# Hybrid decoder block on one Trainium2 core: the PEER gate table's one-hot products in two fp32r passes, with the row-building work shared out anew

## The chip, the cores and the metric

The kernel runs on 1 core of one Trainium2 chip. The metric is the device time in microseconds (us) of one execution. The engines are PE (matmul; PEld is its weight load), DVE (vector), ACT (scalar), POOL (GpSimd) and SP, which issues DMAs.

## The reference, cut to what matters

The block has a mixing sub-layer (projection, gated convolution, windowed attention, output projection) and a channel sub-layer, PEER: every token and each of 8 heads picks 16 of 128 x 128 experts by a product key, softmaxes their scores into gates, and sums the picked experts.

```python
top, pos = lax.top_k(cand, PEER_TOPK)
eidx = jnp.take_along_axis(cidx, pos, axis=-1)       # expert = 128 * ia + ib
g = jax.nn.softmax(top, axis=-1)
a = jax.nn.gelu(jnp.einsum('thkd,td->thk', u_tab[eidx], ht))
return jnp.einsum('thk,thkd->td', g * a, v_tab[eidx])
```

Sizes: 1024 tokens, width 1024, 16384 experts, all in float32. For a token the 8 x 16 = 128 picks are 128 triples (ia, ib, g).

## The kernel before, in words

The 1024 tokens go through the front (norms, projections, attention, output projection, key scores, top 16) in three groups of 384, 384 and 256 tokens (`front`). The first 640 tokens (five tiles of 128) get their experts densely: all 16384 experts are multiplied with the tokens, and a table of gates weights them (`dense`). The last 384 tokens gather their rows by indirect DMA on POOL's queue (`gather`).

`spread` (L714) makes the gate table of one tile of 128 tokens. Its inputs are three [token, pick] arrays, which PE transposes (L720) into PSUM `gps`, so that a pick lies on a partition and a token in a column; ACT copies them to `tr` (L722). For token t the 128 x 128 table is one matmul over the picks: the weights `oi` hold, for pick p, the gate g at column ia; the moving operand `oj` holds a 1 at column ib. A **step** handles four tokens; a tile has 32 steps, the five tiles have 160.

- `make(k)` builds `oi` for four tokens and one `oj` of 4 x 128 columns on DVE (L742). The four tokens' `oi` go by the pattern `HOT = "APVV"`: one on ACT in two instructions (L735, L736), one on POOL and two on DVE, each in one instruction (L738) that compares the column numbers `iota` with ia and multiplies by g. There are 8 `oi` buffers, two steps' worth.
- `multiply(k)` is four fp32 matmuls of 128 columns into one of two PSUM buffers `gps` (L750). The trace shows an fp32 matmul as two records, so a step has 8.
- `evict(k)` copies `gps` to `stage` on ACT (L756); after 8 steps a DMA sends it to DRAM `gd` (L758).

The steps of `spread` are background work. `front` calls `bg(us)` in each half of a projection (L296), which hands out steps at `SPREAD = 0.94` per us of projection time; the tiles of the first group are made in the second group's front, those of the second group in the third's, and whatever is left is drained at a front's end, before the next begins. A tile's steps stand between two `select` passes, which find the picks of a tile and are mainly DVE work. Each engine takes its instructions in one fixed order, which a scheduler sets when the program is built: an instruction that waits holds up all behind it on its engine. On POOL the same queue holds the subtractions that make the low parts of the attention's k and q (`kL` L410, `qL` L418) and of the mixed output (`mc` L402).

The core of the step before:

```python
for x in range(4):
    oi = gb.tile([P, P], F32, name="oi", bufs=8)
    who = pat[t % len(pat)]
    ...
        (G if who == "P" else V).tensor_scalar(oi, iota, tr[:, 0, t:t + 1], tr[:, 2, t:t + 1],
                                               op0=ALU.is_equal, op1=ALU.mult)
```

Of the kernel before, what the change touches and what calls it, by code (L numbers as in the profile page):

```python
# [21 lines left out]
P = 128  # L22
# [4 lines left out]
PH = 8  # L27
# [20 lines left out]
GT = 3  # L48
J = 4
TB = 32  # L50
HOT = "APVV"
RATE0, RATE = 0.0, 0.49
ORDER = True
BACK = 0
# [20 lines left out]
def hymba_peer_kernel(ctx: ExitStack, tc: tile.TileContext, a, out: bass.AP):  # L75
# [65 lines left out]
    vpv = t1.tile([P, P], F32, name="vpv")  # L141
    upv = t1.tile([P, 4, 2], F32, name="upv")
    V.memset(upv, 0.0)
    stat = t1.tile([P, 5, P], F32, name="stat")
    nc.sync.dma_start(stat, a["stat"])
    back = t1.tile([P, 5, P], F32, name="back")
    nc.sync.dma_start(back, a["back"])
# [196 lines left out]
    def group_stats(chunks, T):  # L344
        pt = pj.tile([P, TM], F32, name="pj")
        for i, src in enumerate(chunks):
            sq = tmp("sq")[:, 0:T]
            A.activation(sq, src, AF.Square)
            PE.matmul(pt[:, 0:T], stat[:, i, :], sq, start=(i == 0), stop=(i == len(chunks) - 1))
        r = tp.tile([P, TM + 2], F32, name="grs", tag="u", bufs=1)  # L350
        A.activation(r[:, 0:T], pt[:, 0:T], AF.Sqrt, bias=epsc)
        V.reciprocal(r[:, 0:T], r[:, 0:T])

        def bcast(i):
            bp = pj.tile([P, TM], F32, name="pj")
            PE.matmul(bp[:, 0:T], back[:, i, :], r[:, 0:T], start=True, stop=True)
            return bp[:, 0:T]

        return bcast
# [262 lines left out]
    def select(va, iu):  # L622
# [14 lines left out]
        pairs(1, 3, 8, 16)  # L637
        pairs(4, 4, 4, 40)
        pairs(8, 8, 1, 56)
        top = sel.tile([P, PH, 16], F32, name="top")  # L640
        pu = sel.tile([P, PH, 16], U32, name="pu")
        yield
        for m0 in range(0, 8, 4):
# [44 lines left out]
        for s, src in ((0, aab), (1, stb)):  # L688
# [7 lines left out]
            m = 8  # L696
# [16 lines left out]
        V.tensor_copy(gate[:, ti, :], g)  # L713

    def spread(ti, ia, ib, g):
        gb = env["gb"]
        pat = HOT
        tps = gp.tile([P, 3, P], F32, name="gps")
        for k, src in enumerate((ia, ib, g)):
            PE.transpose(tps[:, k, :], src, ident)  # L720
        tr = gb.tile([P, 3, P], F32, name="tr", bufs=2)
        A.copy(tr, tps)  # L722
        ng = gb.tile([P, 2, P], F32, name="ng", bufs=1)
        A.activation(ng, tps[:, 0:3:2, :], AF.Copy, scale=-1.0)
        n, per = P // 4, TB // 4
        made, outs, stages = {}, {}, {}

        def make(k):
            ois = []
            for x in range(4):  # L730
                t = 4 * k + x
                oi = gb.tile([P, P], F32, name="oi", bufs=8)
                who = pat[t % len(pat)]
                if who == "A":
                    A.activation(oi, iota, AF.Abs, bias=ng[:, 0, t:t + 1])  # L735
                    A.activation(oi, oi, AF.Relu, scale=ng[:, 1, t:t + 1], bias=tr[:, 2, t:t + 1])  # L736
                else:
                    (G if who == "P" else V).tensor_scalar(oi, iota, tr[:, 0, t:t + 1], tr[:, 2, t:t + 1],  # L738
                                                           op0=ALU.is_equal, op1=ALU.mult)
                ois.append(oi)  # L740
            oj = gb.tile([P, 4, P], F32, name="oj", bufs=2)
            V.tensor_tensor(oj, iota.unsqueeze(1).to_broadcast([P, 4, P]),  # L742
                            tr[:, 1, 4 * k:4 * k + 4].unsqueeze(2).to_broadcast([P, 4, P]), op=ALU.is_equal)
            made[k] = ois, oj

        def multiply(k):
            ps = outs[k] = gp.tile([P, 4, P], F32, name="gps")
            ois, oj = made.pop(k)
            for x in range(4):
                PE.matmul(ps[:, x, :], ois[x], oj[:, x, :], start=True, stop=True)  # L750

        def evict(k):
            q, r = divmod(k, per)
            if r == 0:
                stages[q] = gat.tile([P, P, TB], F32, name="stage")
            A.copy(stages[q][:, :, 4 * r:4 * r + 4], outs.pop(k).rearrange("p t j -> p j t"))  # L756
            if r == per - 1:
                nc.sync.dma_start(gd[(ti * P - DT0) // TB + q], stages.pop(q))  # L758

        for k in range(-1, n + 1):  # L760
            for step, d in ((make, 1), (multiply, 0), (evict, -1)):
                if 0 <= k + d < n:
                    step(k + d)
            if 0 <= k < n:
                yield
# [329 lines left out]
            drain(t)  # L1095
    gbc = tc.tile_pool(name="gb", bufs=1, side="right")
    env["gb"] = gbc.__enter__()
    for (t0, T), nxt in zip(GROUPS[1:], nxts[1:]):
        prev = add(prev, SPREAD)
        hs, ft = front(t0, T, hs, nxt)  # L1100
        drain(prev)
        prev = ft
# [12 lines left out]
def _layout(i):  # L1115
# [13 lines left out]
    def colm(v):  # L1129
# [4 lines left out]
        i["conv_w"][0].reshape(12, P).T, colm(i["conv_out_g"][0]), colm(i["attn_out_g"][0]),  # L1134
        np.tile(i["q_norm_g"][0], 2)[:, None], np.tile(i["k_norm_g"][0], 2)[:, None],
        np.tile(i["sinks"][0], (P, 1))], axis=1)
    stat = np.zeros((P, 5, P), np.float32)
    for m in range(5):
        stat[0:64, m, 2 * m] = stat[64:128, m, 2 * m + 1] = 1 / 64
    r = np.arange(384)  # L1140
    dist = 255 - r
    ok = (dist >= 0) & (dist < 128)
# [13 lines left out]
        "v": f(i["peer_v"][0]),  # L1156
        "ident": np.eye(P, dtype=np.float32),
        "stat": f(stat),
        "back": f((stat > 0).astype(np.float32).transpose(2, 1, 0)),
# [19 lines left out]
```

## Time and profile before

| | |
|---|---|
| median of 3 runs | 2819.97 us (2813.15 to 2822.08) |
| profiled execution, its own time | 2812.93 us |
| span in its trace | 2811.2 us |
[...]
| busy share of the span | PE 95%, PEld 87%, DVE 81%, ACT 39%, POOL 51% |

The profiled execution is 0.25% under the median of the other runs. About the first 1000 us are the front, the rest is the dense stage with the gather beside it. A busy share is a mean over both, so what a change in the front is worth is read in the stretches in which the tables are made, which lie between 374 and 916 us.

### The profile page before, as it was taken

How to read it: one execution, taken by the hardware profiler on the slowest of the kernel's cores; microseconds unless marked ns; L12 is line 12 of the kernel's file. 1: busy time of each engine (PE TensorE's matmuls, PEld its weight loads, DVE VectorE, ACT ScalarE, POOL GpSimd, SP SyncE). 2: the span in 40 equal slices, each digit the busy share in tenths (PEclk: the TensorE clock that was granted, in tenths of full speed). 3: DMA queues.
4: the chain of work that ended last, by engine and by line, in shares of the span. 5: the costliest groups of instructions: out<-in, count | busy, mean ns of one | idle time of the engine just before them, and what ended most of it. 6: DMA issues, size and time to landing. Idle time of an engine off the chain costs nothing.

```text
span 2811.2 us, 45327 instructions
## 1 busy us (share of the span) xinstructions
PE 2684.1 (95%) x15679; PEld 2443.0 (87%) x15679; DVE 2287.5 (81%) x4845; ACT 1090.8 (39%) x2201; POOL 1439.0 (51%) x1323
## 2 busy tenths in 40 slices
PE   8898999999888889999999999999999999999998
PEld 6777989889788788999989899989988899889997
DVE  3664899777987687888988888888888888898886
ACT  2454479774788433232223222322222222222321
POOL 3443433320333145666666566666665666566661
PEclk7999999999999989999999999999999999999999
DMA  7878755677667868999999999999999999999995
GB/s 243 270 245 283 249 198 197 219 256 247 218 212 276 293 224 288 355 329 330 336 341 337 330 360 332 331 332 346 338 314 326 344 340 338 327 337 335 331 332 178
DMA packets 381445, 830.39 MB, mean 295 GB/s; under 512 B 35328, under 2 KB 134048, under 8 KB 378272
## 3 DMA queue, kind: packets, MB, share of 16 engines
q1 hardware_dynamic: 267456, 415.89, 44.6%
q0 software_dynamic: 112320, 408.99, 40.2%
q8 instruction: 123, 2.02, 0.3%
q10 hardware_dynamic: 1440, 2.62, 0.2%
q14 instruction: 106, 0.87, 0.1%
HBM read 746.10 MB, written 81.26 MB: 294 GB/s over the span
## 4 chain that ended last, share of the span: by engine, by line
PE 67%; DVE 13%; DMA 10%; issue 5%; ACT 3%; POOL 2%; SPq 0%; DVEq 0%; ACTq 0%; POOLq 0%
PE pv L921 25%; PE pa L864 23%; PE pj L301 10%; DMA vraw<-in_v 4%; PE gps L750 4%; DMA wraw<-in_wq 2%; DVE pq L816 1%; DVE vdL L908 1%; DVE rows L808 1%; PE pj L310 1%; PE po L477 1%; PE pm L195 1%; DMA rows<-in_u,eidx 1%; DVE gw L883 1%; DMA wt<-in_w_ada 1%
## 5 line engine op out<-in xcount | busy, mean ns | idle before, releaser
L864 PE MATMUL pa<-h,uH 128*128 128x320 f32 x4096 | 776.2, 312 | 16.0 <-ACT uH L847 6.0
L864 PEld LDWEIGHTS pa<-h,uH 128*128 128x128 f32 x4096 | 652.1, 190 | 23.7 <-ACT uH L847 7.0
L921 PE MATMUL pv<-vdH,wdH 128*128 128x512 f32 x1275 | 500.4, 393 | 18.3 <-DVE dacc L940 17.7
L921 PE MATMUL pv<-vdL,wdH 128*128 128x512 f32 x1275 | 498.9, 391 | 0.1
L921 PE MATMUL pv<-vdH,wdL 128*128 128x512 f32 x1275 | 497.9, 390 | 0.0
L864 PE MATMUL pa<-h,uL 128*128 128x320 f32 x2048 | 471.1, 312 | 3.7 <-POOL uL L848 3.7
L848 POOL TENSOR_TENSOR uL<-uraw,uH 128x512 fp32r<-128x512 f32 x256 | 342.3, 1338 | 153.3 <-ACT uH L847 142.7
L789 POOL DMA_INDIRECT rows<-in_u,eidx x257 | 260.7, 1015 | 206.4 <-DVE aw L808 102.7
L738 POOL TENSOR_SCALAR oi<-iota,tr 128x128 f32<-128x128 f32 x160 | 156.0, 976 | 386.1 <-PE gps L750 203.5
L864 PEld LDWEIGHTS pa<-h,uL 128*128 128x128 f32 x2048 | 346.3, 190 | 4.6 <-POOL uL L848 4.6
L789 POOL DMA_INDIRECT rows<-in_v,eidx x254 | 254.9, 1003 | 169.1 <-DVE pq L816 119.4
L940 DVE TENSOR_TENSOR dacc<-dacc,pv 128x512 f32<-128x512 f32 x310 | 212.4, 685 | 147.0 <-PE pv L921 133.5
L816 DVE SCALAR_TENSOR_TENSOR pq<-rows,aw,pq 128x1024 f32<-128x1024 f32 x253 | 324.9, 1284 | 3.8 <-DMA rows<-in_v,eidx 1.1
L907 ACT CAST vdH<-vraw 128x512 fp32r<-128x512 f32 x255 | 153.0, 619 | 445.6 <-DMA vraw<-in_v 393.5
L808 DVE CUSTOM_DVE_ANT_0 rows<-rows,pq 128x1024 f32<-128x1024 f32 x257 | 307.8, 1214 | 11.8 <-issue 8.8
L921 PEld LDWEIGHTS pv<-vdH,wdH 128*128 128x128 f32 x1275 | 240.5, 189 | 73.4 <-DVE dacc L940 24.3
L847 ACT CAST uH<-uraw 128x512 fp32r<-128x512 f32 x256 | 158.2, 619 | 368.0 <-DMA uraw<-in_uT 296.5
L921 PEld LDWEIGHTS pv<-vdH,wdL 128*128 128x128 f32 x1275 | 240.5, 189 | 50.8
L921 PEld LDWEIGHTS pv<-vdL,wdH 128*128 128x128 f32 x1275 | 240.4, 189 | 47.7 <-DVE vdL L908 0.6
L890 ACT CAST wdH<-gw 128x640 fp32r<-128x640 f32 x128 | 93.1, 728 | 424.5 <-DVE gw L883 388.0
L908 DVE TENSOR_TENSOR vdL<-vraw,vdH 128x512 fp32r<-128x512 f32 x255 | 192.8, 773 | 79.7 <-ACT vdH L907 73.0
L280 ACT CAST wH<-wraw 128x512 fp32r<-128x512 f32 x252 | 154.2, 618 | 161.5 <-PE pj L301 74.8
(257 smaller groups left out, 4965.2 us busy)
## 6 DMA issues: line engine op xcount, KB each, us to landing
uraw<-in_uT SPq DMA_DIRECT2D x256, 256.0 KB
vraw<-in_v SPq DMA_DIRECT2D x255, 256.0 KB
gd<-stage SPq DMA_DIRECT2D x20, 2048.0 KB
gt<-gd SPq DMA_DIRECT2D x160, 256.0 KB
wraw<-in_w_in SPq DMA_DIRECT2D x108, 256.0 KB
wraw<-in_wq SPq DMA_DIRECT2D x96, 256.0 KB
wt<-in_w_ada SPq DMA_DIRECT2D x40, 512.0 KB
wL<-low_w_in SPq DMA_DIRECT2D x72, 256.0 KB
```

What stands on the lines that cost most here:

```text
L280: A.copy(wH, w)
L301: PE.matmul(pt[:, 0:T], wl[:, c, :], sr[h][:, c, 0:T], start=(h == 0 and c == 0 and k == 0), stop=(h == 1 and c == 3 and k == 2))
L738: (G if who == "P" else V).tensor_scalar(oi, iota, tr[:, 0, t:t + 1], tr[:, 2, t:t + 1], op0=ALU.is_equal, op1=ALU.mult)
L789: G.indirect_dma_start(out=r, out_offset=None, in_=table, in_offset=bass.IndirectOffsetOnAxis(ap=eidx[:, ti, k:k + 1], axis=0))
L808: V.tensor_tensor_reduce(out=r, in0=r, in1=h2, op0=ALU.mult, op1=ALU.add, scale=1.0, scalar=0.0, accum_out=aw[:, k:k + 1])
L816: V.scalar_tensor_tensor(acc, r, aw[:, k:k + 1], acc, op0=ALU.mult, op1=ALU.add)
L847: A.copy(uH, raw)
L848: G.tensor_tensor(uL, raw, uH.bitcast(F32), op=ALU.subtract)
L864: PE.matmul(AT[j][:, s, 0:n], l[:, c, :], h2[r][4 * h + c][:, s * n:s * n + n], start=(h == 0 and c == 0 and k == 0), stop=(h == 1 and c = ...
L908: V.tensor_tensor(vL, raw, vH.bitcast(F32), op=ALU.subtract)
L921: PE.matmul(pt, l[:, P * tt:P * tt + P], r, start=(m == 0), stop=(m == 3 * J - 1))
L940: V.tensor_tensor(dst, dst, pt, op=ALU.add)
```

## The change

The gate is split into a high part, rounded to fp32r, and the rest; the weights become two matrices per token (`oi[:, 0]` with the high part, `oi[:, 1]` with the low), and a token's table is two fp32r matmuls that add up in PSUM, in place of one fp32 matmul. All `oi`, `oj` are fp32r. Of the four tokens of a step:

- tokens 0 and 1: DVE compares both at once in bf16 (`hots`, 256 columns), then writes their four weight matrices in one multiplication (`two`, 512 columns, two buffers);
- token 2: POOL, two instructions (one per part);
- token 3: POOL, two instructions, in even steps; ACT, four instructions (Abs, Relu, and a scaled copy per part) in odd steps.

Tokens 2 and 3 share three `oi` buffers of both parts, that is one and a half steps' worth. Per tile there are two more ACT copies and one DVE subtraction. Beside it the statistics weights `stat` shrink from 5 x 128 columns to 136 that are read at shifted places, `top` shares a buffer tag with `bits`, and a bf16 copy of `iota` is made once.

```diff
-        tr = gb.tile([P, 3, P], F32, name="tr", bufs=2)
-        A.copy(tr, tps)
-        ng = gb.tile([P, 2, P], F32, name="ng", bufs=1)
-        A.activation(ng, tps[:, 0:3:2, :], AF.Copy, scale=-1.0)
+        tr = gb.tile([P, 2, P], F32, name="tr", bufs=1)
+        A.copy(tr, tps[:, 0:2, :])
+        parts = gb.tile([P, 2, P], F32, name="parts", bufs=1)
+        A.copy(parts[:, 0, :].bitcast(F32R), tps[:, 2, :])
+        V.tensor_tensor(parts[:, 1, :], tps[:, 2, :], parts[:, 0, :], op=ALU.subtract)
+        tri = gb.tile([P, P], BF16, name="tri", bufs=1)
+        A.copy(tri, tps[:, 0, :])
...
         def make(k):
+            hots = gb.tile([P, P, 2], BF16, name="hots", bufs=1)
+            V.tensor_tensor(hots, iotas, tri[:, t:t + 2].unsqueeze(1).to_broadcast([P, P, 2]), op=ALU.is_equal)
+            two = gb.tile([P, 2, 2, P], F32R, name="two", bufs=2)
+            V.tensor_tensor(two, hots.rearrange("p i x -> p x i").unsqueeze(1).to_broadcast([P, 2, 2, P]),
+                            parts[:, :, t:t + 2].unsqueeze(3).to_broadcast([P, 2, 2, P]), op=ALU.mult)
+            ois = [two[:, :, x, :] for x in range(2)]
+            for x in (2, 3):
                 t = 4 * k + x
-                oi = gb.tile([P, P], F32, name="oi", bufs=8)
+                oi = gb.tile([P, 2, P], F32R, name="oi", bufs=3)
+                if x == 3 and k % 2:
+                    one = gb.tile([P, P], F32, name="one", bufs=1)
+                    A.activation(one, iota, AF.Abs, scale=-1.0, bias=tr[:, 0, t:t + 1])
+                    A.activation(one, one, AF.Relu, scale=-1.0, bias=ones[:, 0:1])
+                    for s in range(2):
+                        A.activation(oi[:, s, :], one, AF.Copy, scale=parts[:, s, t:t + 1])
                 else:
+                    for s in range(2):
+                        G.tensor_scalar(oi[:, s, :], iota, tr[:, 0, t:t + 1], parts[:, s, t:t + 1],
+                                        op0=ALU.is_equal, op1=ALU.mult)
...
             for x in range(4):
-                PE.matmul(ps[:, x, :], ois[x], oj[:, x, :], start=True, stop=True)
+                for s in range(2):
+                    PE.matmul(ps[:, x, :], ois[x][:, s, :], oj[:, x, :], start=(s == 0), stop=(s == 1))
```

How the program's order moves, engine by engine. First POOL, in the second group's front, from the last projection split (`wL`) of the first group to the third tile's rows; before, and then with the change (`kL`, `qL` and `mc` as above).

```order
L284 TENSOR_TENSOR wL<-wraw,wH 128x512 x45
L738 TENSOR_SCALAR oi<-iota,tr 128x128 x12
L410 TENSOR_TENSOR kL<-k,kH 128x384
L418 TENSOR_TENSOR qL<-y,qH 128x384 x4
L738 TENSOR_SCALAR oi<-iota,tr 128x128 x46
L402 TENSOR_TENSOR mc_4173<-y,mc_4172 128x384 x4
L738 TENSOR_SCALAR oi<-iota,tr 128x128 x45
```

```order
L283 TENSOR_TENSOR wL<-wraw,wH 128x512 x45
L749 TENSOR_SCALAR oi<-iota,tr,parts 128x128 x36
L409 TENSOR_TENSOR kL<-k,kH 128x384
L417 TENSOR_TENSOR qL<-y,qH 128x384 x4
L749 TENSOR_SCALAR oi<-iota,tr,parts 128x128 x140
L401 TENSOR_TENSOR mc_4304<-y,mc_4303 128x384 x4
L749 TENSOR_SCALAR oi<-iota,tr,parts 128x128 x118
```

Ahead of `kL` and `qL`, of which the attention's score matmuls read, stand 36 row instructions (12 steps) where there were 12.

Second, PE at the first steps of the first tile, before and with the change; before, a step is x4, with the change it is x4 of `two` and x4 of `oi`.

```order
L349 MATMUL pj<-sq,stat 128x384
L750 MATMUL gps<-oj,oi 128x128 x8
L349 MATMUL pj<-sq,stat 128x384 x2
L750 MATMUL gps<-oj,oi 128x128 x8
L301 MATMUL pj<-hL_2228,wH 128x384
L301 MATMUL pj<-hH_2226,wL 128x384
```

```order
L348 MATMUL pj<-sq,stat 128x384 x2
L762 MATMUL gps<-oj,two 128x128 x8
L762 MATMUL gps<-oj,oi 128x128 x8
L348 MATMUL pj<-sq,stat 128x384
L762 MATMUL gps<-oj,two 128x128 x4
L762 MATMUL gps<-oj,oi 128x128 x4
L762 MATMUL gps<-oj,two 128x128 x4
L762 MATMUL gps<-oj,oi 128x128 x4
L762 MATMUL gps<-oj,two 128x128 x4
L762 MATMUL gps<-oj,oi 128x128 x4
L300 MATMUL pj<-hH_2226,wL 128x384
```

The table's matmuls still come in bursts between the projection's; the first burst now has five steps behind one another where it had two and two.

Third, DVE at the same place.

```order
L742 TENSOR_TENSOR oj<-iota,tr 128x512
L738 TENSOR_SCALAR oi<-iota,tr 128x128 x2
L742 TENSOR_TENSOR oj<-iota,tr 128x512
L738 TENSOR_SCALAR oi<-iota,tr 128x128 x2
L612 MAX top<-cand 128x8 x6
```

```order
L753 TENSOR_TENSOR oj<-iota,tr 128x512
L724 TENSOR_TENSOR parts<-gps,parts 128x128
L753 TENSOR_TENSOR oj<-iota,tr 128x512
L733 TENSOR_TENSOR hots<-iotas,tri 128x256
L611 MAX top<-cand 128x8
L735 TENSOR_TENSOR two<-hots,parts 128x512
L611 MAX top<-cand 128x8
```

Every DVE instruction of a step now reads two tensors; the TENSOR_SCALARs, which read one, are gone.

## Rows read from the trace of the kernel before

**Rows 1.** The page: busy time by engine, and the chain that ended last, by line.
```profile
PE 2684.1 (95%) x15679; PEld 2443.0 (87%) x15679; DVE 2287.5 (81%) x4845; ACT 1090.8 (39%) x2201; POOL 1439.0 (51%) x1323
PE pv L921 25%; PE pa L864 23%; PE pj L301 10%; DMA vraw<-in_v 4%; PE gps L750 4%; DMA wraw<-in_wq 2%; DVE pq L816 1%; DVE vdL L908 1%; DVE rows L808 1%; PE pj L310 1%; PE po L477 1%; PE pm L195 1%; DMA rows<-in_u,eidx 1%; DVE gw L883 1%; DMA wt<-in_w_ada 1%
```
**Rows 2.** Busy time by stretch, five tiles' stretches: first, last, sum.
```profile
374.00:448.00 74.00, 72.17 (x502) 65.25 (x500) 71.20 (x246) 66.55 (x166) 40.45 (x37) 1.00 0.47 169
...
820.00:916.00 96.00, 85.26 (x645) 79.91 (x644) 76.29 (x237) 73.70 (x171) 35.77 (x38) 0.96 0.71 242
sum 420.50, PE 391.68 PEld 357.88 DVE 352.17 ACT 350.29 POOL 175.49; mean PE 78.34 PEld 71.58 DVE 70.43 ACT 70.06 POOL 35.10
```
**Rows 3.** The same stretches, L738 alone (DVE, then POOL): first tile, sum.
```profile
374.00:448.00 74.00, 20.05 (x64) 35.51 (x32) 1.00 0.47 169
...
sum 420.50, DVE 105.62 POOL 155.98; mean DVE 21.12 POOL 31.20
```
**Rows 4.** Busy time by stretch, L750 alone (PE, PEld): first tile's four bursts.
```profile
376.50:392.60 16.10, 10.30 (x80) 9.43 (x79) 1.00 0.25 81
401.00:411.10 10.10, 8.16 (x64) 7.63 (x64) 1.00 0.36 129
418.30:430.30 12.00, 7.88 (x64) 7.49 (x64) 1.00 0.30 98
438.80:447.60 8.80, 5.88 (x48) 5.66 (x48) 1.00 0.30 93
```
**Rows 5.** All instructions in these four bursts: their sum.
```profile
sum 47.00, PE 46.43 PEld 43.23 DVE 46.35 ACT 45.42 POOL 30.42; mean PE 11.61 PEld 10.81 DVE 11.59 ACT 11.35 POOL 7.60
```
**Rows 6.** Groups by line and shape: busy us, mean ns | idle before.
```profile
L738 POOL TENSOR_SCALAR oi<-iota,tr 128x128 f32<-128x128 f32 x160 | 156.0, 976 | 386.1 <-PE gps L750 203.5 <-ACT tr L722 169.9 <-DVE mx L453 7.5
...
L742 DVE TENSOR_TENSOR oj<-iota,tr 128x512 f32<-128x512 f32 x160 | 111.6, 703 | 13.2 <-PE gps L750 12.3 <-ACT tr L722 0.6
L738 DVE TENSOR_SCALAR oi<-iota,tr 128x128 f32<-128x128 f32 x320 | 105.6, 368 | 28.5 <-PE gps L750 27.2
...
L698 DVE TENSOR_TENSOR hot<-hot 128x256 bf16<-128x256 bf16 x16 | 4.6, 288 | 0.3
...
L736 ACT ACTIVATE oi<-oi,tr,ng 128x128 f32<-128x128 f32 x160 | 76.1, 491 | 1.2
L735 ACT ACTIVATE oi<-iota,ng 128x128 f32<-128x128 f32 x160 | 64.1, 402 | 14.4 <-PE gps L750 13.6
```
**Rows 7.** Instructions in order of time (start us, us), POOL and DVE, three places.
```profile
374.53 2.49 POOL L738 TENSOR_SCALAR oi<-iota,tr 128x128 f32<-128x128 f32 x2 [35.91 <-ACT tr L722]
...
407.18 1.41 DVE L738 TENSOR_SCALAR oi<-iota,tr 128x128 f32<-128x128 f32 x4
...
407.72 0.79 POOL L738 TENSOR_SCALAR oi<-iota,tr 128x128 f32<-128x128 f32 x1 [0.22 <-PE gps L750]
...
442.14 2.85 POOL L738 TENSOR_SCALAR oi<-iota,tr 128x128 f32<-128x128 f32 x2 [0.34 <-PE gps L750]
...
443.12 1.29 DVE L742 TENSOR_TENSOR oj<-iota,tr 128x512 f32<-128x512 f32 x2
```
**Rows 8.** The chain in order of time (start us, us): two steps of the table.
```profile
401.24 1.78 PE gps L750 x16
```
**Rows 9.** Instructions in order of time: fp32r matmuls of 128, 256, 384 columns.
```profile
901.28 0.27 PE L544 MATMUL pm<-identr,h2H 128*128 128x128 f32 x1
...
902.06 0.28 PE L544 MATMUL pm<-identr,h2L 128*128 128x128 f32 x1
...
902.34 0.28 PE L301 MATMUL pj<-h2L,wH 128*128 128x256 f32 x1
...
902.81 0.28 PE L301 MATMUL pj<-h2H,wL 128*128 128x256 f32 x1
...
444.15 0.34 PE L301 MATMUL pj<-hH,wL 128*128 128x384 f32 x1
...
445.54 0.34 PE L301 MATMUL pj<-hL,wH 128*128 128x384 f32 x1
```

More of the change, by code (lines that the diff above doesn't have):

```diff
@@ L50 @@
 TB = 32
-HOT = "APVV"
 RATE0, RATE = 0.0, 0.49
@@ L143, in hymba_peer_kernel @@
     V.memset(upv, 0.0)
-    stat = t1.tile([P, 5, P], F32, name="stat")
+    stat = t1.tile([P, 8 + P], F32, name="stat")
     nc.sync.dma_start(stat, a["stat"])
@@ L348, in group_stats @@
             A.activation(sq, src, AF.Square)
-            PE.matmul(pt[:, 0:T], stat[:, i, :], sq, start=(i == 0), stop=(i == len(chunks) - 1))
+            PE.matmul(pt[:, 0:T], stat[:, 8 - 2 * i:8 - 2 * i + P], sq, start=(i == 0), stop=(i == len(chunks) - 1))
         r = tp.tile([P, TM + 2], F32, name="grs", tag="u", bufs=1)
@@ L639, in select @@
         pairs(8, 8, 1, 56)
-        top = sel.tile([P, PH, 16], F32, name="top")
+        top = sel.tile([P, PH, 16], F32, name="top", tag="bits", bufs=2)
         pu = sel.tile([P, PH, 16], U32, name="pu")
@@ L715, in spread @@
     def spread(ti, ia, ib, g):
-        gb = env["gb"]
-        pat = HOT
+        gb, iotas = env["gb"], env["iotas"]
         tps = gp.tile([P, 3, P], F32, name="gps")
@@ L728, in make @@
         def make(k):
-            ois = []
-            for x in range(4):
-                t = 4 * k + x
-                oi = gb.tile([P, P], F32, name="oi", bufs=8)
[L733 to L736, printed above, removed]
-                else:
-                    (G if who == "P" else V).tensor_scalar(oi, iota, tr[:, 0, t:t + 1], tr[:, 2, t:t + 1],
-                                                           op0=ALU.is_equal, op1=ALU.mult)
+            t = 4 * k
+            hots = gb.tile([P, P, 2], BF16, name="hots", bufs=1)
[5 more added lines that the diff above has]
+            for x in (2, 3):
+                t = 4 * k + x
+                oi = gb.tile([P, 2, P], F32R, name="oi", bufs=3)
[5 more added lines that the diff above has]
+                        A.activation(oi[:, s, :], one, AF.Copy, scale=parts[:, s, t:t + 1])
+                else:
+                    for s in range(2):
+                        G.tensor_scalar(oi[:, s, :], iota, tr[:, 0, t:t + 1], parts[:, s, t:t + 1],
+                                        op0=ALU.is_equal, op1=ALU.mult)
                 ois.append(oi)
-            oj = gb.tile([P, 4, P], F32, name="oj", bufs=2)
+            oj = gb.tile([P, 4, P], F32R, name="oj", bufs=2)
             V.tensor_tensor(oj, iota.unsqueeze(1).to_broadcast([P, 4, P]),
@@ L1097, in hymba_peer_kernel @@
     env["gb"] = gbc.__enter__()
+    env["iotas"] = env["gb"].tile([P, P, 2], BF16, name="iotas")
+    A.copy(env["iotas"], iota.unsqueeze(2).to_broadcast([P, P, 2]))
     for (t0, T), nxt in zip(GROUPS[1:], nxts[1:]):
@@ L1136, in _layout @@
         np.tile(i["sinks"][0], (P, 1))], axis=1)
-    stat = np.zeros((P, 5, P), np.float32)
+    stat = np.zeros((P, 8 + P), np.float32)
+    stat[0:64, 8] = stat[64:128, 9] = 1 / 64
+    back = np.zeros((P, 5, P), np.float32)
     for m in range(5):
-        stat[0:64, m, 2 * m] = stat[64:128, m, 2 * m + 1] = 1 / 64
+        back[2 * m, m, 0:64] = back[2 * m + 1, m, 64:128] = 1
     r = np.arange(384)
@@ L1158, in _layout @@
         "stat": f(stat),
-        "back": f((stat > 0).astype(np.float32).transpose(2, 1, 0)),
+        "back": back,
         "iota": f(np.broadcast_to(np.arange(P, dtype=np.float32), (P, P))),
```

## The prediction

> **What bounds the kernel now.** The page comes first: PE is busy for 95% of the span, and the chain that ended last runs mostly through PE, 4% of it through the table's matmuls at L750 [rows 1]. A stall of PE in the front therefore lengthens the kernel, and the dense stage behind it only moves. So the question is what PE waits for while tables are made. Busy time by stretch answers it: the five tiles take 420.5 us, in which PE is busy for 391.7, DVE for 352.2, ACT for 350.3 and POOL for 175.5 [rows 2], of which 156.0 are the 160 row instructions of L738 [rows 3]. Inside a tile the steps come in bursts. The first tile has four, of 10, 8, 8 and 6 steps (8 records each), and they take 16.1, 10.1, 12.0 and 8.8 us [rows 4]. In these 47.0 us PE, DVE and ACT are each busy for 45 to 46, POOL for 30 [rows 5]: three engines are in balance, POOL alone has room. What POOL waits for is room in the row buffers: 203.5 us of its idle time end with L750 [rows 6].
>
> **The change part by part.**
>
> *PE: nothing.* Two steps of fp32 matmuls take 1.78 us, 0.89 a step, 0.111 for each of the 16 records [rows 8]. An fp32r matmul of 128 columns starts 0.78 us before the seventh one after it, 0.111 apart (first and last of the eight between 901.28 and 902.06) [rows 9]. Eight such passes a step are 0.89 us again. fp32r matmuls of 256 columns stand 0.118 apart (the first and fifth of five) and of 384 columns 0.174 (the first and ninth of nine) [rows 9], so below 256 columns the spacing hardly falls any more.
>
> [...]
>
> *DVE: +41 us of work, +0 on the path.* A step loses two L738 at 0.368 and keeps `oj` at 0.703. It gains `hots`, 256 columns of bf16, nearest row 0.288 (L698), and `two`, 512 columns with mixed types, nearest row `oj` itself, 0.703 [rows 6]. From 1.44 to 1.69 us a step, times 160. The cover is the 420.5 - 352.2 = 68.3 us that DVE is idle in the five stretches [rows 2], and the longer bursts below; without it the 41 would be paid.
>
> *ACT: +0.* Before, each step has 0.402 + 0.491; now every second step has four instructions between these two values, 1.6 to 2.0 us, or 0.8 to 1.0 a step [rows 6].
>
> *POOL: the term that decides.* Two steps now need six row instructions (four in the even, two in the odd) where they needed two: 480 instead of 160. What does one cost? Alone beside DVE's L738 it takes 0.79 us; beside DVE's L742, which reads two tensors, pairs take up to 2.85 us (L742 of 443.12 falls into it), another 2.49, that is 1.42 and 1.24 each [rows 7]. The mean of all 160 is 0.976 [rows 6], that of the first tile, where DVE is busiest, 35.51/32 = 1.11 [rows 3]. With the change DVE's step is two-tensor work only. That the output is fp32r and the second scalar another column I cost at nothing: the ends 0.79 and 1.24 hold that. I take 1.05, between the mean and the first tile's.
>
> [...]
>
> Now a burst. Three instructions a step; the three buffers (two instructions each) let POOL enter a burst with six done, if the pause before is long enough. The pauses in the first tile are 8.4, 7.2 and 8.5 us (the ends and beginnings of the bursts) [rows 4], six instructions at 1.05 take 6.3. So a burst of n steps lasts (3n - 6) x 1.05 where POOL sets the pace: 24 x 1.05 = 25.2 for 16.1 us, 18 x 1.05 = 18.9 for 10.1 and for 12.0, 12 x 1.05 = 12.6 for 8.8. The excess is 9.1 + 8.8 + 6.9 + 3.8 = 28.6 us a tile and **143 us** for five. The later tiles' bursts are looser (their stretches are up to 96 us long), so their excess is smaller; on the other side the new order puts steps closer together than the old one, and a step's fourth row can be begun only when the third row of the step before has been multiplied. I let these two cancel.
>
> The same by occupancy: 480 x 1.05 = 504 and POOL's other 19.5 us are 524 us in stretches that have 420.5, so at least 103 us must be added even if POOL never waits again. At 0.976 that is 67, at 0.79 nothing.
>
> *What waits behind POOL.* `kL` and `qL` stand behind 36 row instructions where they stood behind 12, and attention's score matmuls stand behind them on PE. That is time within the burst's, not beside it, since PE is held by the steps then; it would be extra if PE passed them. DVE waits at `two` (two buffers) as it waited at `oi`. The 28.8 us that PE is idle in the five stretches [rows 2] can swallow some of the delay, and what piles up on DVE and ACT behind a burst gives some back; I cost the two at nothing together. PE's granted clock is 1.00 in the first stretch and 0.96 in the last, where PE is idle for 11 us [rows 2]; more idle time may bring more of that, within the range.
>
> *Small things.* Two more copies and a subtraction at a tile's start, each under 0.6 us by their neighbours' rows, before POOL may begin: 5 x 0.6 = **3 us**. The smaller `stat` and the shared tag: nothing, one load at the start and a buffer long free.
>
> **The sum.** 143 + 3 = 146 us on the profiled execution's 2812.9: **2959 us**. That execution is 0.25% under the median of 2820.0, within the 0.3% that a measurement of this kernel can tell from no change.
>
> **The range.** The price of a row instruction sets it. At 0.79 the four bursts give 2.9 + 4.1 + 2.2 + 0.7 = 9.9 a tile, 49 in all: 2862. At 1.24 they give 13.7 + 12.2 + 10.3 + 6.1 = 42.3, 211 in all, with the 3 us: 3027. I give **2862 to 3027**.
>
> **The rivals.**
>
> 1. *Faster: a pass costs half.* If two passes of one moving operand run at the spacing that the line through 256 and 384 columns gives at 128, 0.118 - 0.056 = 0.062, a token costs 0.124 for 0.223, and 640 tokens save 63 us; and if POOL fills the pauses and hides, that is 2750 us. For it: PE sets the end. Against it: the rows of 128 columns at 0.111, and bursts in which DVE and ACT are full too, so that PE's saving there would buy little. It decides only where POOL's three instructions take less than a step's 1.2 to 1.6 us of now, under 0.5 each, and no row is under 0.79. Chance 0.05.
> 2. *POOL hides.* At 0.79 its 379 + 19.5 = 399 us fit in the 420.5. If the scheduler's order spreads the steps over the pauses, nothing is left but the 3 us and some DVE: 2815 to 2862 us. Against it: the new order on PE, with five steps in a row at the first tile. Chance 0.07, of which 0.03 within 0.3%.
> 3. *A jam.* If POOL is not ahead when a burst begins, because its queue is held by `kL` and `qL` that wait for ACT, or because the third row's buffer comes free late, every step costs three instructions: at 1.11, 32 x 3.33 = 106.6 for 47.0 us, 59.6 a tile, 298 in all: 3114 us. Against it: pauses of over 7 us between bursts. Chance 0.08.
>
> **Chances.** The forecast with its range 0.80, the rivals 0.05, 0.07 and 0.08. Faster by over 0.3%: 0.05 (the first rival). Within 0.3%: 0.03 (the better part of the second). Slower: 0.92.
>
> **What would show it.** Right: POOL's busy time in the tables' stretches rises from 156 to about 500 us at 1.0 to 1.1 us an instruction; the five stretches grow from 420 to about 565 us together; PE's longest wait in the front is for POOL's `oi`, which it never was before; DVE and ACT are less busy in the bursts than now; PE's spacing in the table stays at 0.111; the dense stage is as long as before. Wrong: row instructions well under 0.9 us, or PE waiting for DVE's `two` rather than POOL's `oi`, or table matmuls 0.06 apart.

## The result: 3057 us for 2820, and the profile after

The median is 3056.66 us (3050.81 to 3062.43, four runs) beside 2820.04 of the kernel before: ratio 1.0848, 95% interval 1.0820 to 1.0876, or 237 us more. The direction is the predicted one; the time lies 98 us over the forecast and 30 over the top of its range. The profiled execution took 3051.56 us, span 3049.8, mean granted clock 0.921 (0.979 before).

The page of the changed kernel: busy time by engine, the chain that ended last, and the group of POOL's rows (busy us, mean ns | idle before).

```profile
PE 2853.8 (94%) x15679; PEld 2586.8 (85%) x15679; DVE 2365.9 (78%) x4850; ACT 1092.8 (36%) x2207; POOL 1786.9 (59%) x1643
PE pv L933 24%; PE pa L876 21%; PE pj L300 11%; POOL oi L749 9%; PE gps L762 3%; DMA vraw<-in_v 2%; DVE pq L828 2%; DMA wraw<-in_wq 1%; DMA wraw<-in_w_in 1%; DVE vdL L920 1%; PE pj L309 1%; PE pm L448 1%; DMA uraw<-in_uT 1%; PE po L476 1%; PE pm L194 1%
L749 POOL TENSOR_SCALAR oi<-iota,tr,parts 128x128 fp32r<-128x128 f32 x480 | 499.7, 1052 | 292.3 <-ACT parts L723 185.1
```

POOL's rows, which were not among the chain's main entries [rows 1], are 9% of it now, some 275 us. PE has as many instructions as before, 15,679, and yet is busy for 170 us more. Busy time by stretch, front and dense stage, first of the changed kernel, then of the kernel before (columns: stretch, its length, PE, PEld, DVE, ACT, POOL busy, granted clock, DMA share, GB/s):

```profile
337.00:1175.00 838.00, 720.40 (x3869) 656.05 (x3868) 573.22 (x1963) 440.76 (x1057) 527.16 (x508) 0.78 0.48 165
1175.00:3049.00 1874.00, 1831.77 (x10278) 1668.56 (x10276) 1603.66 (x2397) 510.39 (x847) 1120.06 (x1031) 0.99 0.93 324
```

```profile
337.00:930.00 593.00, 551.28 (x3830) 512.87 (x3829) 490.19 (x1913) 437.89 (x1047) 180.29 (x185) 0.98 0.67 232
930.00:2811.00 1881.00, 1833.59 (x10279) 1668.80 (x10278) 1601.28 (x2397) 509.64 (x846) 1115.72 (x1030) 0.99 0.93 322
```

All of the loss is in the front, where the tables are made: 838 us for 593, while the dense stage is 7 us shorter. Of the 245 us PE is idle for 76 more ((838 - 720.4) - (593 - 551.3)) and busy for 169 more with the same instructions (to 1%), at a granted clock of 0.78 for 0.98.

The changed kernel's five tiles' stretches, which answer to [rows 2], and the first tile's four bursts, which answer to [rows 4, 5], all instructions:

```profile
383.00:507.00 124.00, 102.24 (x441) 89.49 (x441) 89.87 (x298) 60.69 (x155) 102.40 (x100) 0.64 0.25 89
...
sum 628.00, PE 523.66 PEld 465.90 DVE 423.34 ACT 333.66 POOL 506.20; mean PE 104.73 PEld 93.18 DVE 84.67 ACT 66.73 POOL 101.24
...
384.00:412.50 28.50, 21.14 (x89) 18.25 (x87) 22.54 (x79) 12.94 (x30) 27.83 (x28) 0.61 0.10 38
423.10:447.40 24.30, 17.02 (x72) 15.08 (x70) 18.36 (x38) 10.71 (x29) 24.25 (x21) 0.59 0.05 23
458.70:477.60 18.90, 15.41 (x70) 13.03 (x67) 16.58 (x65) 9.71 (x24) 17.57 (x19) 0.58 0.27 93
489.00:506.00 17.00, 14.72 (x86) 13.98 (x86) 8.00 (x17) 11.46 (x35) 11.08 (x12) 0.70 0.10 32
```

In the first two bursts POOL is busy from end to end (27.8 of 28.5, 24.3 of 24.3) and DVE and ACT, once full, have room. The bursts take 28.5, 24.3, 18.9 and 17.0 us where the prediction had 25.2, 18.9, 18.9 and 12.6, and the granted clock is 0.58 to 0.70 where it was 1.00. Two matmuls of the table in order of time (start us, us), and the waits of 330 to 1180 us (us, count, us of the longest):

```profile
407.55 0.41 PE L762 MATMUL gps<-oj,oi 128*128 128x128 f32 x1
407.76 0.41 PE L762 MATMUL gps<-oj,two 128*128 128x128 f32 x1
```

```profile
POOL oi L749 <- PE gps L762: 107.1, 46, 15.7
PEld gps L762 <- POOL oi L749: 94.8, 117, 2.8
PE gps L762 <- POOL oi L749: 71.7, 104, 2.7
```

PE waits for POOL's rows, as forecast, but its passes stand 0.21 us apart, not 0.111 [rows 9].

### The profile page after: what moved, and what is told of

The parts are those of the page before. It is cut to its first block, busy times and chain, and to the rows that moved or that the text cites. A ratio compares the mean times of both kernels' runs of the same rounds, so it can differ in the third digit from the quotient of the medians.

```text
span 3049.8 us, 45805 instructions
## 1 busy us (share of the span) xinstructions
PE 2853.8 (94%) x15679; PEld 2586.8 (85%) x15679; DVE 2365.9 (78%) x4850; ACT 1092.8 (36%) x2207; POOL 1786.9 (59%) x1643
## 4 chain that ended last, share of the span: by engine, by line
PE 64%; POOL 10%; DVE 9%; DMA 8%; issue 6%; ACT 2%; SPq 1%; DVEq 0%; POOLq 0%; ACTq 0%
PE pv L933 24%; PE pa L876 21%; PE pj L300 11%; POOL oi L749 9%; PE gps L762 3%; DMA vraw<-in_v 2%; DVE pq L828 2%; DMA wraw<-in_wq 1%; DMA wraw<-in_w_in 1%; DVE vdL L920 1%; PE pj L309 1%; PE pm L448 1%; DMA uraw<-in_uT 1%; PE po L476 1%; PE pm L194 1%
## 5 line engine op out<-in xcount | busy, mean ns | idle before, releaser
L749 POOL TENSOR_SCALAR oi<-iota,tr,parts 128x128 fp32r<-128x128 f32 x480 | 499.7, 1052 | 292.3 <-ACT parts L723 185.1
L762 PE MATMUL gps<-oj,oi 128*128 128x128 f32 x640 | 177.2, 358 | 78.9 <-POOL oi L749 71.7
```

The source lines that it names most:

```text
L749: G.tensor_scalar(oi[:, s, :], iota, tr[:, 0, t:t + 1], parts[:, s, t:t + 1], op0=ALU.is_equal, op1=ALU.mult)
L762: PE.matmul(ps[:, x, :], ois[x][:, s, :], oj[:, x, :], start=(s == 0), stop=(s == 1))
```

## The experiments

Two theories stood at first. **Theory 1**, the prediction's: POOL's 480 rows pace the bursts, and all of the loss is theirs. **Theory 2**: two fp32r passes of 128 columns in place of an fp32 matmul let PE's granted clock fall, and that makes the rest. Every run stood beside runs of the kernel before; their medians were 2816 to 2817 us, and its single runs lie between 2805 and 2827. Of e1 to e10, e13 and e14 there is one run each, so a difference of some 10 us says nothing there.

### Which part of the change makes the loss

**e1, POOL builds only the high part** of its rows, the second pass multiplies it again.

```diff
-                    for s in range(2):
-                        G.tensor_scalar(oi[:, s, :], iota, ..., parts[:, s, t:t + 1], ...)
+                    G.tensor_scalar(oi[:, 0, :], iota, ..., parts[:, 0, t:t + 1], ...)
+                    oi = oi[:, 0:1, :].to_broadcast([P, 2, P])
```

> The changed kernel, with POOL building the high part of its rows alone; the low pass multiplies the same matrix again, so the low part of the gate is left out for those tokens and their high part counts twice. POOL's row instructions fall from 480 to 240, PE's fp32r passes stay. Theory 1 (POOL paces the bursts, PE idles in them, and its granted clock falls with the idling): 1.5 instructions of about 1.05 us a step are under a step's share of the stretch, so nearly all comes back: 2830 to 2880 us, granted clock in the five stretches 0.95 or more. Theory 2 (fp32r passes of 128 columns themselves let the clock fall, whatever POOL does): the clock stays under 0.9 there and the time at 2900 to 2960 us.

Measured: 2970.61 us, granted clock 0.81 between 400 and 900 us; POOL's 240 rows at 1209 ns are 290 us. That is 91 us over theory 1's range and 11 over theory 2's. Half of POOL's rows gone bring 86 us of the 237. So the rows matter, but something else is left.

**e2, the kernel before with POOL's row made three times**: 480 POOL instructions, fp32 matmuls, eight buffers.

```diff
+                    for _ in range(3 if who == "P" else 1):
                         (G if who == "P" else V).tensor_scalar(oi, iota, ...)
```

> The kernel before, with each of POOL's rows written three times over by the same instruction: 480 row instructions on POOL, fp32 matmuls, eight row buffers. Theory 1: POOL's load alone makes the loss, clock included: 2990 to 3060 us, granted clock 0.7 to 0.85 in the five stretches. Theory 2: POOL's pace alone costs what was forecast, 2930 to 2960 us, with the clock at 0.95 or more, since fp32 matmuls keep it up.

Measured: 2965.91 us, +149. Its group of POOL's rows:

```profile
L739 POOL TENSOR_SCALAR oi<-iota,tr 128x128 f32<-128x128 f32 x480 | 448.2, 938 | 266.8 <-ACT tr L722 167.1 <-PE gps L751 65.4 <-ACT oi L736 3.1
```

POOL's rows alone are worth 149 us, close to the prediction's 143; it isn't the whole. The time is 6 us over theory 2's range, and its clock missed: between 400 and 900 us it is 0.88 here, with fp32 matmuls, where the kernel before has 0.98, and PE is busy for 414 of the 500 us instead of 467 (both rows stand behind e3's, below). So the 149 us aren't waits alone.

**e3, the kernel before with fp32r operands and two passes of the same rows**: POOL, DVE and ACT do no more than before.

```diff
-                oi = gb.tile([P, P], F32, name="oi", bufs=8)
+                oi = gb.tile([P, P], F32R, name="oi", bufs=8)
...
-                PE.matmul(ps[:, x, :], ois[x], oj[:, x, :], start=True, stop=True)
+                for s in range(2):
+                    PE.matmul(ps[:, x, :], ois[x], oj[:, x, :], start=(s == 0), stop=(s == 1))
```

> The kernel before, with rows and ones in fp32r and each token multiplied in two fp32r passes of the same rows (the gate is rounded and counts twice, the low part is left out); no row instruction is added. Theory 1: 2810 to 2840 us, granted clock in the stretches as before (0.96 to 1.00), passes 0.111 us apart. Theory 2: 2880 us or more, with a clock under 0.9 there.

Measured: 2933.75 us, +116, as theory 2 had it (over 2880, clock under 0.9), from a part that the prediction had priced at nothing. Busy time by 2 us in the first burst of e3 (columns as above):

```profile
378.00:380.00 2.00, 1.95 (x14) 1.55 (x13) 2.00 (x15) 2.00 (x7) 1.70 (x2) 1.00 0.26 99
380.00:382.00 2.00, 0.72 (x7) 0.58 (x6) 2.00 (x16) 2.00 (x6) 0.88 (x2) 1.00 0.09 12
382.00:384.00 2.00, 1.08 (x8) 0.97 (x8) 2.00 (x10) 1.41 (x4) 0.63 (x1) 1.00 0.36 123
384.00:386.00 2.00, 1.01 (x6) 0.85 (x6) 2.00 (x14) 1.31 (x3) 1.46 (x2) 0.66 0.00 0
386.00:388.00 2.00, 1.65 (x8) 1.68 (x9) 1.98 (x14) 0.43 (x2) 0.03 (x1) 0.50 0.00 0
...
392.00:394.00 2.00, 2.00 (x10) 2.00 (x10) 2.00 (x11) 1.84 (x7) 1.16 (x2) 0.50 0.00 0
...
402.00:404.00 2.00, 2.00 (x17) 2.00 (x16) 1.97 (x6) 1.41 (x3) 0.70 (x1) 1.00 1.01 393
```

and PE's instructions there in order of time:

```profile
382.57 1.08 PE L751 MATMUL gps<-oj,oi 128*128 128x128 f32 x8 [1.85 <-ACT stage L757]
384.07 1.01 PE L751 MATMUL gps<-oj,oi 128*128 128x128 f32 x6 [0.42 <-ACT oi L736]
...
394.87 3.70 PE L751 MATMUL gps<-oj,oi 128*128 128x128 f32 x16
...
399.12 0.52 PE L301 MATMUL pj<-hH,wH 128*128 128x384 f32 x1
...
402.22 0.34 PE L301 MATMUL pj<-hH,wL 128*128 128x384 f32 x1
```

PE comes out of full work at 1.00, waits twice between table passes (for ACT's eviction and ACT's row), and the clock goes to 0.50. It stays there with PE busy, 2.00 of 2.00 at 392 to 394, while table passes (and some statistics matmuls) run, 16 passes taking 3.70 us where 16 records of the kernel before take 1.78 at 1.00 [rows 8]. It is back at 1.00 at 402, after the projection's 384-column passes have run without a break since 398.4. In the kernel before the clock falls too, but seldom and not for long (four times, 28 us together, in the table below). Over 400 to 900 us the kernels read, before and then e3 and e2:

```profile
400.00:900.00 500.00, 466.55 (x3279) 434.55 (x3278) 415.40 (x1544) 380.74 (x915) 155.59 (x160) 0.98 0.67 231
```

```profile
400.00:900.00 500.00, 450.83 (x2633) 417.96 (x2632) 347.74 (x1332) 315.47 (x735) 119.59 (x128) 0.84 0.54 185
```

```profile
400.00:900.00 500.00, 413.88 (x2461) 375.78 (x2460) 325.96 (x1246) 288.70 (x684) 314.08 (x337) 0.88 0.51 174
```

e3's PE is busy for 451 of 500 us, e2's for 414, and e3's clock is the lower one. So it isn't idle time alone. Cut into slices of 2 us from 370 us to each kernel's last table matmul, and counting the slices whose granted clock is below 0.97 as whole ones, the runs compare so (e5 to e8 follow below):

| | low stretches | us in them |
|---|---|---|
| before | 4 | 28 |
| e2, fp32, POOL's pace | 24 | 208 |
| e3, two passes of 128 columns | 20 | 246 |
| e8, two passes of 256 columns | 8 | 44 |
| e5, one pass of 128 columns | 14 | 122 |
| e6, one pass of 256 columns | 13 | 126 |
| the change | 30 | 416 |
| e7, the change with 256 columns | 33 | 292 |

All 20 low stretches of e3, all 24 of e2 and the 4 of the kernel before begin behind a slice in which PE was busy for less than 1.8 of the 2 us, in the change 26 of 30; how long they last differs from kernel to kernel: 12 us on the average in e3, where PE is busy for 91% of them, 9 in e2, 14 in the change and 9 in e7. At the lower level the passes are no dearer than the fp32 records they replace: both stand 0.21 us apart there, fp32r in e3 (the 16 in 3.70 us) and fp32 in the kernel before, whose clock is 0.50 from 616 to 622 us:

```profile
616.63 3.78 PE L750 MATMUL gps<-oj,oi 128*128 128x128 f32 x16 [3.64 <-ACT stage L756]
```

Both stand 0.11 apart at 1.00 [rows 8, 9]. So it is the time spent at the lower level that differs.

e3 isn't the passes alone, though. The scheduler set PE's and ACT's instructions in another order, and the table matmuls wait 85.5 us for ACT's evictions where they waited 30.7; the run doesn't part the two.

**e4, the change with four extra fp32r matmuls of 512 columns a step** to keep PE at work.

```diff
+            for _ in range(FILL):
+                PE.matmul(ps, ois[0][:, 0, :], oj, start=True, stop=True)
```

> [...] Theory 1 with its second half (the fallen clock costs as much again as the waiting): the granted clock in the stretches rises from 0.64 to 0.80 to over 0.9, and the time falls to 2960 to 3020 us although PE has more to do. If the clock costs little: no fall, 3050 to 3200 us.

Measured: 3108.82 us, 52 more than the change. The granted clock rose (mean 0.956, and 0.90 for 0.79 between 400 and 900 us), but the extra matmuls, 640 of them, are PE work of some 145 us at clock 1.00, an estimate from the dense stage of the kernel before, where matmuls of 512 columns (L921) start 0.227 us apart; 93 of that were hidden or won back. The expected fall missed, and the run can't say how much of the 93 was clock: inconclusive.

### Does the number of columns in a pass decide

In these kernels a pass multiplies two tokens' columns of `oj` at a time and writes 256 columns; the second half is overwritten by the next token's pass. A step's last token keeps 128, so 1.75 times the columns run in all. The weights, their loads and the number of passes stay.

```diff
+                w = min(x + 2, 4)
-                    PE.matmul(ps[:, x, :], ois[x], oj[:, x, :], ...)
+                    PE.matmul(ps[:, x:w, :], ois[x], oj[:, x:w, :], ...)
```

**e5 and e6, the kernel before with fp32r operands and one pass**, of 128 columns and of 256.

> The kernel before, with its rows and ones in fp32r and one fp32r pass of 128 columns per token (the low part of the gate is left out); 640 passes of 0.111 us in place of 640 fp32 matmuls of 0.223, 71 us less PE work at full clock. Theory 2 (a run of 128-column fp32r passes lets the granted clock fall although PE waits for nothing): the clock falls in the bursts as in the run with two passes, and eats the gain: 2800 to 2870 us, clock 0.85 to 0.95 in the stretches. Theory 3 (what the two passes lost was not the clock but waits for ACT's evictions in another order): half the passes, half the loss or a gain, with the clock near 1: 2750 to 2800 us.

> As the run with one pass of 128 columns, but each token's pass (but a step's last) streams 256 columns, its own and the next token's, and the next token's pass overwrites the second half: the same number of instructions, the same values, 0.117 us instead of 0.111 at full clock. Theory 2: streaming twice the columns in the same time keeps the clock up, so this is faster than the run of 128 columns by 30 us or more: 2750 to 2800 us, clock 0.97 or more in the stretches. Theory 3: the same as the run of 128 columns, within 10 us.

Measured: 2807.42 and 2809.55 us, clock 0.91 between 400 and 900 us in both. With one pass PE is busy for 441 and 447 of these 500 us, where the kernel before has 467, and DVE and ACT, which feed it, for as long as there (414 and 378 in e5, 415 and 381 before); the width makes no difference, neither to the time nor to the low stretches (122 and 126 us): theory 2's 30 us missed. e5 seemed to gain 10 us on the kernel before; e15 below takes that back.

**e7, the change with passes of 256 columns.**

> The changed kernel, with each fp32r pass (but those of a step's last token) streaming 256 columns as above; the values are those of the change. Theory 2: the part of the loss that the passes make goes, POOL's part stays, as in the run of before with POOL's rows tripled: 2950 to 2980 us, clock in the stretches about 0.9. Theory 1 (POOL's pace and the idling alone): 3040 to 3070 us, clock as in the change, 0.64 to 0.80.

Measured: 3028.35 us, 28 less than the change, clock 0.85 for 0.79 between 400 and 900 us. Neither theory's number: the width is worth 28 us here, not 80 to 100. Its waits:

```profile
PEld gps L763 <- POOL oi L749: 125.0, 164, 2.5
PE gps L763 <- POOL oi L749: 91.1, 149, 2.3
```

PE waits longer for POOL (91.1 for 71.7 us): the low stretches are as many as in the change, but shorter (table above), and what the passes win by that is mostly waited out behind POOL.

**e8, e3 with passes of 256 columns.**

> The kernel before with two fp32r passes of the same rows, as in the third run, but 256 columns a pass. Theory 2: the 116 us of the third run go, 2815 to 2850 us, clock in the stretches 0.95 or more. Theory 3: 2910 to 2950 us as in the third run, with PE waiting some 85 us for ACT's evictions again.

Measured: 2854.97 us, 79 less than e3 and 5 over theory 2's range, with 1.75 times the columns; clock 0.98 between 400 and 900 us:

```profile
400.00:900.00 500.00, 460.36 (x3100) 421.70 (x3100) 402.01 (x1506) 363.50 (x870) 151.41 (x153) 0.98 0.63 216
```

Where POOL isn't the bound, the wider passes bring back the clock (0.98 for e3's 0.84) and 79 of e3's 116 us. The other 38 stay open. 9 of them at most are the wider spacing, 1280 x (0.118 - 0.111) [rows 9]; PE waits more for ACT's evictions than before, e8 first and then the kernel before:

```profile
PEld gps L752 <- ACT stage L759: 31.2, 41, 4.1
PE gps L752 <- ACT stage L759: 16.5, 18, 3.9
```

```profile
PEld gps L750 <- ACT stage L756: 18.1, 21, 3.8
PE gps L750 <- ACT stage L756: 12.6, 9, 3.6
```

No run tried that by itself, and the scheduler's order is another in e8 than in e3 or the kernel before: a part of the 79 and of the 38 us may be the order's.

### What is left: how far ahead POOL can work, and its price

e2's 149 and e7's 28 leave about 60 of 237 us. The candidate is the look-ahead, that is, how many steps' rows can be ready before PE has used them: three row buffers for tokens 2 and 3 are one and a half steps' work, where before each token's row had two.

**e9, e7 with five row buffers**; `two` has one buffer instead of two, to make room. **e13, the same on the change as it is** (128 columns).

```diff
-            two = gb.tile([P, 2, 2, P], F32R, name="two", bufs=2)
+            two = gb.tile([P, 2, 2, P], F32R, name="two", bufs=1)
...
-                oi = gb.tile([P, 2, P], F32R, name="oi", bufs=3)
+                oi = gb.tile([P, 2, P], F32R, name="oi", bufs=5)
```

> The changed kernel with 256 columns a pass (3028 us) and five row buffers instead of three, paid for by one buffer of `two` instead of two: POOL may run two and a half steps ahead. If the short look-ahead costs the 62 us by which that kernel is over the kernel before with POOL's rows tripled (eight buffers): 2970 to 2995 us. If POOL's time per instruction does it (1.06 us there, 0.94 in the tripled run): 3015 to 3040 us, with POOL's price unchanged.

> The changed kernel as it is (passes of 128 columns), with five row buffers instead of three and one buffer of `two` instead of two. If the look-ahead's 51 us add to the rest: 2995 to 3015 us. If the low clock fills what the look-ahead frees: 3025 to 3060 us, with the clock in the stretches no higher than in the change.

Measured: 2977.20 us, 51 less than e7; 3008.95 us, 48 less than the change. e13's waits:

```profile
PEld gps L762 <- POOL oi L749: 52.2, 78, 2.0
PE gps L762 <- POOL oi L749: 37.3, 66, 1.9
```

PE's waits for POOL halve (37.3 for 71.7, 52.2 for 94.8), with POOL's work unchanged. e9, in which width and buffers are both changed, is 161 us over the kernel before, against e2's 149 for POOL's rows alone. `two` had one buffer less in both runs, so the 51 and 48 us are the net of the two.

**e14, e2 with six `oi` buffers instead of eight**, so look-ahead shortened where the matmuls are fp32.

> The kernel before with POOL's rows written three times (2966 us), with six row buffers instead of eight: one and a half steps of look-ahead instead of two, fp32 matmuls, no other part of the change. If the look-ahead decides where POOL sets the pace: 2985 to 3025 us. If not: 2955 to 2980 us.

Measured: 2998.86 us, 33 more than e2; PE's wait for POOL is 113.2 us, in e2 89.0. The look-ahead costs without fp32r passes as well.

**e10, the change with DVE's rows made by four TENSOR_SCALARs** (one tensor read) instead of `hots` and `two`.

```diff
-            V.tensor_tensor(hots, ...)
-            V.tensor_tensor(two, ...)
+                    V.tensor_scalar(two[:, s, x, :], iota, tr[:, 0, ...], parts[:, s, ...], ...)
```

> The changed kernel with `hots` and `two` undone: DVE writes the four matrices of tokens 0 and 1 in four TENSOR_SCALARs that read one tensor, at 0.37 us each, 1.47 us for the 1.06 of hots and two, 65 us more DVE work in all. Theory 4 (DVE's two-tensor instructions are what raises POOL's price, and POOL's price is what counts): POOL's row instruction falls from 1.05 to 0.90 to 0.98 us and the time from 3057 to 3000 to 3035 us, although DVE has more to do. If DVE's own work counts: 3060 to 3130 us.

Measured: 3023.92 us, 33 less than the change. The groups, e10 and then the change:

```profile
L749 POOL TENSOR_SCALAR oi<-iota,tr,parts 128x128 fp32r<-128x128 f32 x480 | 473.7, 999 | 292.0 <-ACT parts L723 187.8 <-PE gps L762 92.2 <-ACT wH L279 10.7
L735 DVE TENSOR_SCALAR two<-iota,tr,parts 128x128 fp32r<-128x128 f32 x640 | 192.8, 371 | 51.4 <-PE gps L762 50.8
```

```profile
L735 DVE TENSOR_TENSOR two<-hots,parts 128x512 fp32r<-128x512 bf16 x160 | 114.6, 716 | 74.4 <-PE gps L762 72.0
L733 DVE TENSOR_TENSOR hots<-iotas,tri 128x256 bf16<-128x256 bf16 x160 | 55.0, 344 | 1.9
```

DVE works 23 us more (192.8 for 114.6 + 55.0; 65 had been expected), POOL 26 us less, and the kernel is faster: what DVE saves in the change is paid by POOL, which is the one waited for. The time lies in theory 4's range; the price, 0.999 us, fell by less than its 0.90 to 0.98.

### Three versions with one pass

**e12, the change with the high part alone and one pass. e11, e5 with more rows on POOL and fewer on DVE. e15, e5's kernel once more, with twelve runs.**

> The change with the high part alone: bf16 comparison for two tokens, POOL and ACT rows of one part, one pass of 128 columns, six row buffers; the low part is left out. POOL has 240 instructions, ACT three per odd step, DVE 1.4 to 1.5 us a step as before, PE half. If POOL's count is what made the loss: 2790 to 2830 us, as the one-pass kernel with the rows of before (2807). If the bf16 rows or the order cost of their own: over 2840 us.

> A candidate: one fp32r pass per token (the low part left out), and in every second step the row that ACT made goes to POOL (pattern APVVPPVV): ACT 0.45 us a step less, POOL 0.5 instructions a step more, 240 in all. If waits for ACT's evictions hold the one-pass kernel (60 us of PE waiting for them): 2780 to 2805 us. If POOL's pace comes in instead: 2810 to 2850 us.

> The kernel before with one fp32r pass of 128 columns per token (the low part of the gate is left out), timed in rounds: 0.2 to 0.6% faster than the kernel before, as in the single look (2807 for 2817). Theory: 71 us of PE work saved, most of it given back, since the clock is 0.91 there and DVE and ACT are full in the bursts.

Measured: e12 2817.51 us, ratio 1.0000 (0.9983 to 1.0018), POOL's 240 rows at 1224 ns; e11 2839.40 us, 1.0089 (1.0062 to 1.0115), rows at 1082 ns; e15 2814.58 us, 1.0002 (0.9985 to 1.0018). e5's 10 us below the kernel before, from one run, were not real. None beats the kernel before: a pass less on PE buys nothing there, as the prediction's first rival had against it (DVE and ACT are full in the same bursts); besides, the clock between 400 and 900 us is lower (0.92 in e15, 0.90 in e12, 0.87 in e11, for 0.98). In e11 80 more POOL rows than in e15 (240 for 160) cost 25 us. In e12 POOL has the same 240 rows, at a higher price, and they cost nothing; its POOL and ACT rows have six buffers, three steps' worth, where e11's eight for all rows are two. DVE's rows differ too, so this doesn't show the look-ahead by itself.

## Why the prediction was right in sign and short in size

The runs that changed a part measured 149 us for POOL's rows (e2), 48 for the short look-ahead (e13) and 28 for the width of the passes (e7), together 225 of 237. That this nearly adds up is chance, for the parts overlap: the passes alone cost 116 us on the kernel before (e3), which with e2's 149 is already 265, and half of POOL's rows gone bring 86 (e1). What they share is the clock. Busy time by stretch in the fronts of e1, e2 and e3 (columns as above; each up to some 42 us before the dense stage's first matmul, as in the two rows further up):

```profile
337.00:1083.00 746.00, 673.54 (x3847) 625.46 (x3845) 558.40 (x1943) 434.99 (x1053) 314.79 (x267) 0.82 0.54 184
337.00:1090.00 753.00, 623.26 (x3844) 569.24 (x3843) 502.38 (x1919) 444.21 (x1048) 471.45 (x506) 0.89 0.54 183
337.00:1053.00 716.00, 636.84 (x3831) 591.38 (x3829) 498.90 (x1923) 453.69 (x1046) 174.75 (x185) 0.85 0.56 192
```

| front, against the kernel before | longer | PE idle | PE busy | full-speed time lost to the clock (estimate) |
|---|---|---|---|---|
| the change | 245 | +76 | +169 | +172 |
| e1, the change with half of POOL's rows | 153 | +31 | +122 | +122 |
| e2, POOL's rows alone | 160 | +88 | +72 | +71 |
| e3, the passes alone | 123 | +37 | +86 | +96 |

The last column is worked out from the rows: the stretch times (1 - granted clock), less the 12 us of the kernel before (593 x 0.02). It comes to what PE is busy longer, within 10 us in e3 and 3 us elsewhere. So by this estimate over two thirds of the change's loss in the front, 169 of 245 us, are PE doing the same work at the lower clock, and 76 us are longer waits. The 169 aren't the passes' alone: with POOL's rows alone (e2) the clock of the front is 0.89 for 0.98 as well.

**POOL, the deciding term: right in price and work, lucky in its total.** The price of 1.05 us a row was measured at 1.052, POOL's busy time 499.7 us, and PE waits for the rows as forecast. 143 + 3 us stands beside e2's 149, but by two errors against each other: e2's rows cost 0.938 us, at which the prediction's bursts give 20.6 us a tile, 103 in all, and 72 of the 160 us in e2's front are PE busy at the lower clock, which the sum had not. e10 bears out the reason given for the price, that rows beside DVE's two-tensor instructions are slow: with fewer of these the rows fall to 0.999 us. The change's trace shows it row by row: the 116 rows with no TENSOR_TENSOR of DVE beside them take 0.79 us on the average, the 157 beside which DVE's TENSOR_TENSOR records add up to 0.8 us or more 1.40.

**DVE and ACT at nothing: right.** Both are less busy in the bursts than before, and no long wait of PE is for `two`. But DVE's share has a side that the step left out: its new form raises POOL's price, 33 us by e10.

**"PE: nothing" failed.** The working took the spacing of 0.111 us from rows at granted clock 1.00 [rows 8, 9] and assumed that level for the changed kernel. That fp32 and fp32r cost the same holds at either level (0.11 us at 1.00, 0.21 at 0.50); the level does not. In the change a pass takes 0.21 us at clock 0.50, PE is busy 169 us longer in the front, and the same edit on the kernel before costs 116 us with no more work for the other engines (e3). The prediction's half sentence on the clock, "more idle time may bring more of that, within the range", put at nothing what became the largest part of the loss: 416 us of low clock in the change, 28 in the kernel before. Idle time does stand ahead of the fall, as it said (in all 20 low stretches of e3), but behind it the passes of 128 columns run on at 0.50 with PE busy (e3); with wider passes the low stretches shrink (e8: 44 us for e3's 246; e7: 292 for the change's 416), though not where there is one pass a token (e6: 126 for e5's 122).

**"I let these two cancel" failed.** Looser later tiles were set against "a step's fourth row can be begun only when the third row of the step before has been multiplied". The second was worth 48 us (e13) and 51 (e9). The six instructions that POOL was to have done when a burst begins were the best case, too: ACT's row of an odd step takes one of the same three buffers, so a burst that begins with an odd step finds four. In the first tile the four bursts are 88.7 us together where 75.6 were forecast, and the pauses between them grew from 24.1 us to 33.3, 22 us over the forecast. The later tiles were looser, as said: all five stretches are 62 us over the forecast, not five times 22. Another 37 us of the front's growth lie outside the stretches. What of this is short look-ahead and what the low clock in the bursts (0.58 to 0.70) the runs don't part. The prediction's third rival, the jam at 3114 us, named a buffer that "comes free late" as its cause; the time came a little over half way to it. (The range's lower end, 2862, leaves out the sum's 3 us; nothing hangs on it.)

**What the prediction said would show it.** POOL at 500 us and 1.0 to 1.1 each: yes. PE's longest wait in the front for POOL's `oi`: yes. The five stretches at about 565 us: they are 628. The spacing at 0.111: no, it is 0.21 where the clock is at 0.50 (0.112 at 1.00, the median), and this was the line that pointed at the missed term. The dense stage as long as before: 1874 for 1881. **The first rival** (half the passes' cost) and **the second** (POOL hides) are out: the passes didn't get cheaper, and e2 pays 149 us for as many rows.

## What to carry to other kernels

When a matmul is replaced by passes of another type, an equal spacing at full clock isn't enough: here the spacings were equal at both of PE's levels (0.11 and 0.21 us), and the loss came from the time spent at the lower one. Look at the granted clock of the stretch and at PE's busy time for the same instructions, and work out what falling to the lower level there would cost. When work is moved to an engine with room, price three things apart: its pace in the bursts, the number of its buffers in steps of work (not in tiles), and what the moved instructions' neighbours on other engines do to their duration (here 0.79 to 1.40 us). Here the room was 245 us of POOL in five stretches, and it was spent at the bursts' pace, not at the mean.

## What was not expected of the hardware

- Behind a wait, fp32r passes of 128 columns went on at clock 0.50 although PE was busy without a gap (e3, 392 to 394 us: 2.00 of 2.00 at 0.50); the clock rose in the projection's 384-column passes (0.50 from 398 to 400 us, 1.00 from 402 to 404). With passes of 256 columns e3's edit had 44 us of low clock for 246, and was 79 us faster with 1.75 times the columns (e8). With one pass a token the width changed nothing (e5, e6: 122 and 126 us of low clock, 2807 and 2810 us). What in the narrow passes makes the difference, and what in the program's order, the runs don't tell.
- One and the same POOL instruction, a TENSOR_SCALAR of 128 x 128, took from 0.79 us [rows 7] through 0.94 (e2), 1.00 (e10) and 1.05 (the change) to 1.21 (e1) and 1.22 (e12) as a mean. By and large it goes with what DVE's TENSOR_TENSOR records beside the rows add up to, as a share of the rows' time: 29% in e2, 33% in e10, 58% in the change, 78% in e1, 82% in e12 (41% at 0.976 in the kernel before).
